# Four token mixers after a two-layer block: the stream kept by token, and the first mixer's branches as a pipeline

## The chip, the cores and the metric

One core of a Trainium2 chip runs the whole program once. The metric is device time in microseconds (us) of one execution. TensorE is PE in the views (PEld is its weight load), VectorE is DVE, ScalarE is ACT, GpSimd is POOL, SyncE (which issues the transfers) is SP.

## What is computed

The program has two parts. The first (two attention and expert layers) is untouched. The second, "block 2", runs four mixers over a stream `h` of 256 tokens with 1024 channels, all in float32:

```
for i in range(4):
    u = rms_norm_2(h, norm_pre[i])
    y = (nsa_mixer, diff_mixer, dilated_mixer, stick_mixer)[i](u, ...)
    h = h + rms_norm_2(y, norm_post[i])
```

Each mixer projects `u` by `w_in` into queries, keys, values and a gate `z`, attends, and returns `(o * silu(z)) @ w_out`. The first (`nsa`) has 16 heads in 4 groups that share keys, and sums three branches per head with weights from a sigmoid gate: attention over 15 compressed blocks, over selected blocks (here all of the causal past) and over a window (here the same).

## The kernel before

**Stream.** `h` lies by channel: tile `xT`, 128 channels x 8 x 256 tokens. `pre` (L317) makes `u = h * gain * r` by channel and splits it into a high and a low half (`uh`, `ul`), since every projection is three products of rounded halves (`gemm`, L261 to L263). The first projections of a mixer (`values`, L568, products L578) don't wait for `u`: they take `raw`, the halves of `h * gain` without the norm's factor (`raw_split`, L303), and scale the result by token (`rc`). A sum of squares by channel goes through small products with a matrix of 1/1024 (L314, L394).

**Weights.** `wload` (L207) brings 256 columns of a matrix, 1 MB, into one of five buffers; `split` (L234) makes two pairs of halves of it, a cast on ScalarE (L248) and a difference on VectorE (L249) each, in a pool of 4 + 4 tiles (`wh`, `wl`), so two chunks at a time. 48 products of 128x128 by 128x256 use one chunk.

**First mixer** (`nsa`, L770). After the keys and values come 4 groups; in each a chunk of queries, then 2 pairs of heads; for a pair two branches, `br` 1 (selected, with the compressed scores in its first 16 columns) and 0 (window). One branch of a pair, called a step here, is: 12 score products (L436), bias and row maximum on VectorE (L928), exponential with row sum on ScalarE (L930), 6 transposes (L465), 2 copies on ScalarE (L467), 4 products with the values (L475, 8 rows in the trace). The weights 1/sum x gate are applied after the products: spread over 64 columns, transposed (L959), copied (L961) and multiplied with the sum (L962). Compressed weights go through L935 to L948 and L967. `gate_split` (L599) makes the four gate chunks, in program order behind the groups.

**End of a mixer.** `out_proj` (L339) multiplies by `w_out` into channels (L350, L385), 192 products; the norm's sums, then by channel pair `y * r`, `h + y` (L411 to L415, VectorE and GpSimd), the next `raw` (L307, L308) and its squares. The last mixer uses `out_last` (L2164), which works by token: rows of `h` come from 16 transposes (L742).

**Order.** Nothing of this is the order on an engine: a scheduler places every instruction ahead of time, so gate products fill gaps of the groups already. PSUM has 8 banks: 2 `mm`, 5 shared by scores and transposes (`x`), 1 `o`.

Of the kernel before, what the change touches and what calls it, by code (L numbers as in the profile page):

```python
# [10 lines left out]
F32 = mybir.dt.float32  # L11
# [8 lines left out]
S = 256  # L20
# [87 lines left out]
class K:  # L108
# [208 lines left out]
    def pre(self, pool, h, gain):  # L317

        nc = self.nc
        if self.raw is None:  # L320
            self.raw_begin(gain)
            for k in range(KT):
                self.raw_split(h, k)
        r = self.rsqrt(pool, self.raw_ps[:, :S], S)
        p = self.pst()
        for t in range(2):
            nc.tensor.matmul(p[:, t:t + 1], r[0:1, 128 * t:128 * t + 128], self.ones[0:1, 0:1], start=True, stop=True)
        rc = pool.tile([128, 2], F32, name="rcol", tag="rcol")
        nc.vector.tensor_copy(rc, p[:, :2])
        u = pool.tile([128, KT, S], F32, name="u", tag="sq")  # L330
        uh = pool.tile([128, KT, S], F32R, name="uh", tag="uh")
        ul = pool.tile([128, KT, S], F32R, name="ul", tag="ul")
        for k in range(KT):
            nc.vector.scalar_tensor_tensor(u[:, k], h[:, k], gain[:, k:k + 1], r, op0=ALU.mult, op1=ALU.mult)
            nc.scalar.copy(uh[:, k], u[:, k])
            (nc.gpsimd if k % 2 else nc.vector).tensor_sub(ul[:, k], u[:, k], uh[:, k].bitcast(F32))
        return (uh, ul), u, rc, r

    def out_proj(self, pool, h, oh, ol, w_out, gain, ahead):  # L339


        nc = self.nc
        y = pool.tile([128, KT, S], F32, name="y", tag="v")
        sq = pool.tile([128, KT, S], F32, name="ysq", tag="sq")
        ps = self.pst()

        def product(p, w, ks):
            for m, k in [(m, k) for m in range(2) for k in ks]:
                for j, (a, b) in enumerate(((1, oh), (0, ol), (0, oh))):
                    nc.tensor.matmul(p[:, 256 * m:256 * m + 256], w[a][k][:, 128 * m:128 * m + 128], b[:, k],  # L350
                                     start=k == 0 and m == 0 and j == 0, stop=k == KT - 1 and m == 1 and j == 2)

        def evict(p, c):
            v = p.rearrange("p (m n) -> p m n", m=2)
            cs = slice(2 * c, 2 * c + 2)
            nc.scalar.activation(sq[:, cs], v, AF.Square)
            nc.vector.tensor_mul(y[:, cs], v, gain[:, cs].unsqueeze(2).to_broadcast([128, 2, S]))
            if 0 < c < 3:
                nc.gpsimd.tensor_add(sq[:, 0:2], sq[:, 0:2], sq[:, cs])

        weights = lambda c: self.wsplit(w_out[:, 256 * c:256 * c + 256], after=self.oh_last if c == 2 else (), pool_too=c == 1)

        ws, p = [weights(0), weights(1)], [self.mm(), self.mm()]
        for ks in ((0, 1, 2, 3), (4, 5), (6, 7)):
            for c in range(2):
                product(p[c], ws[c], ks)
        for c in range(2):
            evict(p[c], c)
        for c in (2, 3):
            w = weights(c)  # L370
            if c == 3 and ahead is not None:
                raw = [self.wload(a) for a in ahead[0]]
                self.ahead = [self.split(raw[0])]
            if c == 2:
                p = self.mm()
                product(p, w, range(KT))
                evict(p, c)
                nc.gpsimd.tensor_add(sq[:, 0], sq[:, 0], sq[:, 1])
            else:

                p = [self.mm()[:, :S], self.pss()[:, :S]]
                for m, ks in ((0, (0, 1, 2, 3)), (1, (0, 1, 2, 3)), (0, (4, 5, 6, 7)), (1, (4, 5, 6, 7))):
                    for k in ks:
                        for j, (a, b) in enumerate(((1, oh), (0, ol), (0, oh))):
                            nc.tensor.matmul(p[m], w[a][k][:, 128 * m:128 * m + 128], b[:, k],  # L385
                                             start=k == 0 and j == 0, stop=k == KT - 1 and j == 2)
                    if ks[0]:
                        k = 6 + m
                        nc.scalar.activation(sq[:, k], p[m], AF.Square)
                        nc.vector.tensor_scalar(y[:, k], p[m], gain[:, k:k + 1], None, op0=ALU.mult)  # L390
        if ahead is not None:
            half = self.split(raw[1][:, :4])
        for j, k in enumerate((0, 6, 7)):
            nc.tensor.matmul(ps[:, :S], self.onesD, sq[:, k], start=j == 0, stop=j == 2)  # L394
        r = self.rsqrt(pool, ps[:, :S], S)
        self.raw = None
        if ahead is not None:
            self.raw_begin(ahead[1])
        last = None

        def then(f):
            nonlocal last
            if last is None:
                last = f()
            else:
                with self.tc.issue_after(last):
                    last = f()

        for i in range(KT + 2):
            if i < KT:  # L410
                then(lambda: nc.vector.tensor_mul(y[:, i], y[:, i], r).ins)  # L411
                if i % 2 == 0:
                    then(lambda: nc.vector.tensor_add(h[:, i], h[:, i], y[:, i]).ins)
                else:
                    nc.gpsimd.tensor_add(h[:, i], h[:, i], y[:, i])  # L415
            j = i - LAG
            if 0 <= j < KT and ahead is not None:
                then(lambda: self.raw_split(h, j))
                if j == AT:
                    with self.tc.issue_after(last):  # L420
                        self.ahead.append([x + y for x, y in zip(half, self.split(raw[1][:, 4:], pool_too=PT))])
# [47 lines left out]
    def spread(self, po, vs, ats):  # L469


        first = None
        for kt, (of, n) in enumerate(((0, 256), (256, 128))):
            for half, (at, _) in enumerate(ats):
                i = self.nc.tensor.matmul(po[64 * half:64 * half + 64, 256 - n:256], vs[half][kt], at[:, of:of + n],  # L475
                                          start=kt == 0, stop=kt == 1).ins
                first = first or i
        self.behind(first, *(i for _, i in ats))

    def diff(self, h, gpre, gpost, ahead=None):  # L480
# [5 lines left out]
        with ExitStack() as ctx:  # L486
# [3 lines left out]
            u, _, rc, _ = self.pre(pool, h, gpre)  # L490
            v = pool.tile([128, 2, D], F32, name="v", tag="v")
            self.values(rc, self.columns256(w_in, 2048, v))
# [16 lines left out]
            for c in range(4):  # L509
                ops = []  # L510
                for base, sc in ((0, 0.125), (1024, 1.0)):
                    w = self.wsplit(w_in[:, base + 256 * c:base + 256 * c + 256])
                    p = self.mm()
                    hi = wk.tile([128, 2, S], F32R, name="qkh", tag=f"qkh{base}")
                    lo = wk.tile([128, 2, S], F32R, name="qkl", tag=f"qkl{base}")
                    for m in range(2):
                        pm = p[:, 256 * m:256 * m + 256]
                        self.gemm_cm(pm, w, m, u)
                        self.split_ps(hi[:, m], lo[:, m], pm, sc)
# [29 lines left out]
            for c in range(4):  # L549
# [5 lines left out]
                self.sigmoid(sz, pz)  # L555
                nc.vector.tensor_mul(sz, sz, pz)
# [8 lines left out]
            self.out_proj(pool, h, oh, ol, w_out, gpost, ahead)  # L565


    def values(self, rc, parts):  # L568

        nc = self.nc  # L570
        x, (last_a, last_b) = self.raw, self.raw_last
        ps = [self.mm(), self.mm()] + (self.pair() if len(parts) > 2 else [])

        def product(i, w, k):
            for t in range(2):
                ts = slice(128 * t, 128 * t + 128)
                for j, (a, b) in enumerate(((0, 1), (1, 0), (0, 0))):
                    nc.tensor.matmul(ps[i][:, 256 * t:256 * t + 256], x[a][:, k, ts], w[b][k], start=k == 0 and t == 0 and j == 0,  # L578
                                     stop=k == KT - 1 and t == 1 and j == 2)

        ws = self.ahead or [self.wsplit(src) for src, _ in parts[:2]]
        self.ahead = None
        for k in range(KT):
            for i in range(2):
                product(i, ws[i], k)
        for i, (src, v) in enumerate(parts):
            if i > 1:
                with self.tc.issue_after(last_a), self.tc.issue_after(last_b):
                    w = self.wsplit(src)
                for k in range(KT):  # L590
                    product(i, w, k)
# [7 lines left out]
    def gate_split(self, wk, w_in, col, x, o, oh, ol, last=None):  # L599

        nc = self.nc
        for c in range(4):
            w = self.wsplit(w_in[:, col + 256 * c:col + 256 * c + 256])
            sz = wk.tile([128, 512], F32, name="sz", tag="sz")
            pz = self.mm()
            for m in range(2):
                self.gemm_cm(pz[:, 256 * m:256 * m + 256], w, m, x)
            self.sigmoid(sz, pz)
# [1674 lines left out]
```

## Time and profile before

| what | us |
|---|---|
| three runs | 1576.27, 1581.42, 1582.22 |
| median of them | 1581.42 |
| the profiled execution, and its span in the trace | 1575.4, 1573.8 |
| PE, DVE, ACT, POOL busy | 1426.8, 974.1, 809.6, 314.5 |
| block 2: first mixer, second, third, fourth | 911 to 1127.5, to 1276, to 1415.5, to 1573.8 |

Busy PE is a share of time in which some product was under way; products overlap, and at the lower clock one takes twice as long and counts as busy too. So the clock that was granted and the distance from product to product are read beside it.

### The profile page before, as it was taken

To read this page: it belongs to the slowest core of one execution; us is meant where nothing else is said; L and a number is where in the kernel's file an instruction comes from. 1 tells how busy PE (TensorE), PEld (TensorE's weight loads), DVE (VectorE), ACT (ScalarE), POOL (GpSimd) and SP (SyncE) were. 2 spreads that over 40 slices of the span, in tenths; PEclk is the share of its full clock that TensorE was granted. 3 is DMA by queue.
4 is the path that set the end of the run, shared out by engine and by line. 5 is a ranking of instruction groups with operands and counts; after the bars stand their busy time and mean duration, and the time that the engine had idled before them with its cause. 6 is when DMAs were issued, how large, how long until landed. Compare 5 with 4: busy or idle time off the path is not lost.

```text
span 1573.8 us, 26604 instructions
## 1 busy us (share of the span) xinstructions
PE 1426.8 (91%) x10361; PEld 1154.0 (73%) x10361; DVE 974.1 (62%) x2043; ACT 809.6 (51%) x1644; POOL 314.5 (20%) x311
## 2 busy tenths in 40 slices
PE   5989987889599898998799999998999989989998
PEld 3767865566477776767466678775899889979997
DVE  4555669863677556875412366553777776768675
ACT  4455454543366544664212344664456755745574
POOL 2000124322211103111000021322321141322242
PEclk8999999999799998999899999995999999999999
DMA  8700259874699987315799937330354454344520
GB/s 266 236 27 3 94 189 291 260 255 149 212 331 341 348 269 266 106 41 185 245 332 366 344 102 219 107 107 1 113 161 134 135 172 150 129 129 153 160 82 27
DMA packets 243689, 284.71 MB, mean 181 GB/s; under 512 B 14546, under 2 KB 227554, under 8 KB 243556
## 3 DMA queue, kind: packets, MB, share of 16 engines
q1 hardware_dynamic: 236644, 259.85, 50.9%
q0 software_dynamic: 6912, 23.07, 4.5%
q8 instruction: 85, 1.39, 0.4%
q14 instruction: 48, 0.39, 0.1%
HBM read 275.56 MB, written 9.44 MB: 181 GB/s over the span
## 4 chain that ended last, share of the span: by engine, by line
PE 43%; ACT 4%; DVE 2%; POOL 1%; issue 1%; another core or an unknown queue 0%; DVEq 0%; ACTq 0%
PE ps_mm L261 6%; PE ps_mm L263 5%; PE ps_mm L262 5%; PE ps_mm L1992 4%; PE ps_mm L350 3%; PE ps_mm L578 2%; PE ps_x L436 2%; PE ps_x L578 2%; PE ps_t L2032 2%; PE ps_o L475 1%; PE ps_t L1975 1%; ACT wh L248 1%; PE ps_x L465 1%; PE ps_s L2037 1%; PE ps_mm L2175 1%
## 5 line engine op out<-in xcount | busy, mean ns | idle before, releaser
L249 DVE TENSOR_TENSOR wl<-w,wh 128x1024 fp32r<-128x1024 f32 x257 | 321.4, 1258 | 147.0 <-ACT wh L248 143.7
L248 ACT CAST wh<-w 128x1024 fp32r<-128x1024 f32 x261 | 270.0, 1042 | 128.2 <-PE ps_mm L263 59.8
L261 PE MATMUL ps_mm<-uh,wl 128*128 128x256 f32 x720 | 209.3, 291 | 0.0
L262 PE MATMUL ps_mm<-ul,wh 128*128 128x256 f32 x720 | 205.5, 285 | 0.0
L263 PE MATMUL ps_mm<-uh,wh 128*128 128x256 f32 x720 | 204.9, 285 | 0.0
L261 PEld LDWEIGHTS ps_mm<-uh,wl 128*128 128x128 f32 x720 | 136.8, 190 | 4.8 <-issue 1.5
L263 PEld LDWEIGHTS ps_mm<-uh,wh 128*128 128x128 f32 x720 | 136.9, 190 | 1.5 <-issue 0.8
L262 PEld LDWEIGHTS ps_mm<-ul,wh 128*128 128x128 f32 x720 | 137.0, 190 | 1.3 <-issue 0.8
L261 PE MATMUL ps_mm<-wh,xl 128*96 128x256 f32 x256 | 75.8, 296 | 3.5 <-DVE xl L427 3.5
L262 PE MATMUL ps_mm<-wl,xt 128*96 128x256 f32 x256 | 74.2, 290 | 0.0
L263 PE MATMUL ps_mm<-wh,xt 128*96 128x256 f32 x256 | 73.1, 286 | 0.0
L1043 PE MATMUL ps_mm<-w,cond 128*32 128x256 f32 x768 | 55.5, 404 | 15.6 <-DVE mod L1050 9.4
L2074 PE MATMUL ps_s<-w,ht 128*96 128x512 f32 x128 | 57.6, 593 | 0.0
L1992 PE MATMUL ps_mm<-w,xt 128*64 128x256 f32 x384 | 51.5, 384 | 0.0
L261 PE MATMUL ps_mm<-hh,wl 128*128 128x512 f32 (+2 forms) x136 | 47.5, 351 | 2.9 <-DVE qn L1087 2.6
L1043 PEld LDWEIGHTS ps_mm<-w,cond 128*32 128x32 f32 x768 | 22.2, 113 | 37.4 <-DVE mod L1050 12.4
L313 POOL TENSOR_TENSOR rawsq<-rawsq 128x256 f32<-128x256 f32 x16 | 13.7, 857 | 176.7 <-ACT rawsq L312 176.6
L350 PE MATMUL ps_mm<-oh,wl 128*128 128x256 f32 x144 | 42.5, 302 | 6.9 <-DVE sz L609 2.9
L261 PEld LDWEIGHTS ps_mm<-wh,xl 128*96 128x96 f32 x256 | 42.7, 167 | 7.7 <-DVE xl L427 4.5
L262 PE MATMUL ps_mm<-hl,wh 128*128 128x512 f32 (+2 forms) x136 | 47.3, 348 | 0.3 <-DVE hl L1068 0.2
L263 PE MATMUL ps_mm<-hh,wh 128*128 128x512 f32 (+2 forms) x136 | 46.8, 344 | 0.0
L1489 POOL TENSOR_TENSOR xk<-d,KD 128x512 f32<-128x512 f32 x27 | 39.8, 1481 | 33.6 <-PE ps_x L1496 13.2
(654 smaller groups left out, 3998.1 us busy)
## 6 DMA issues: line engine op xcount, KB each, us to landing
w<-mod_w SPq DMA_DIRECT2D x48, 1024.0 KB, 7.3
w<-exp_w_up SPq DMA_DIRECT2D x28, 1024.0 KB, 10.6
w<-exp_w_gate SPq DMA_DIRECT2D x27, 1024.0 KB, 11.9
w<-exp_w_down SPq DMA_DIRECT2D x27, 1024.0 KB, 11.3
w<-b_w_in SPq DMA_DIRECT2D x16, 1024.0 KB, 5.6
w<-d_w_in SPq DMA_DIRECT2D x16, 1024.0 KB, 5.4
w<-a_w_in SPq DMA_DIRECT2D x14, 1024.0 KB, 8.3
w<-c_w_in SPq DMA_DIRECT2D x14, 1024.0 KB, 5.0
```

The source lines that it names most:

```text
L248: nc.scalar.copy(hv, raw[:, i:i + c])
L249: (nc.gpsimd if i and pool_too else nc.vector).tensor_sub(lv, raw[:, i:i + c], hv.bitcast(F32))
L261: nc.tensor.matmul(out, sl(k), mh(k), start=k == ks[0], stop=False)
L262: nc.tensor.matmul(out, sh(k), ml(k), start=False, stop=False)
L263: nc.tensor.matmul(out, sh(k), mh(k), start=False, stop=k == ks[-1])
L350: nc.tensor.matmul(p[:, 256 * m:256 * m + 256], w[a][k][:, 128 * m:128 * m + 128], b[:, k], start=k == 0 and m == 0 and j == 0, stop=k == ...
L436: self.nc.tensor.matmul(out, q[a], k[b], start=j == 0, stop=j == 2)
L578: nc.tensor.matmul(ps[i][:, 256 * t:256 * t + 256], x[a][:, k, ts], w[b][k], start=k == 0 and t == 0 and j == 0, stop=k == KT - 1 and t == ...
L1043: nc.tensor.matmul(p[j:j + 32, :256], self.cond[:, k], w[:, k], start=k < 4, stop=k >= 4)
L1489: nc.gpsimd.tensor_mul(xk, d, Ks)
L1992: nc.tensor.matmul(p[64 * a:64 * a + 64, 256 * j:256 * j + 256], xt[:, k, off + 64 * a:off + 64 * a + 64], w[j][a][k], start=k == 0, stop= ...
L2074: nc.tensor.matmul(p, ht[:, f], w[:, f, cs], start=f == 0, stop=f == 1)
```

## The change

Block 2 keeps `h` by token (`self.h`, filled by 16 transposes inside the first mixer, `rows_of`). `pre`, `u` and its halves are gone: all projections take `raw`, and the norm's factor is multiplied into each result on VectorE (`normed`), from PSUM, before the split. The output product lies by token in all four mixers; `out_last` is merged into `out_proj`. There each token tile (128 tokens) has its own chain: norm, sum, 8 transposes, and the halves of 128 columns at a time for the next mixer. In `nsa` a step's weights are scaled by 1/sum x gate on VectorE before they are turned, so both branches, both pairs and the compressed part add up in one bank (`po[g]`), which is multiplied by the gate once. The steps are written as a pipeline, scores of the next ahead of the transposes of this one, and each group has its gate chunk inside. `gain` of the output norm is now a row, loaded for each mixer.

```diff
+    def norm_first(self):
+        nc.scalar.activation(self.rr, self.raw_ps[:, :S], AF.Ln, bias=self.eps)
+        nc.scalar.activation(self.rr, self.rr, AF.Exp, scale=-0.5)
         p = self.pst()
         for t in range(2):
+            nc.tensor.matmul(p[:, t:t + 1], self.rr[0:1, 128 * t:128 * t + 128], self.ones[0:1, 0:1], start=True, stop=True)
...
+    def normed(self, wk, p, r, n=2):
+        t = wk.tile([128, n, S], F32, name="normed", tag="normed")
+        self.nc.vector.tensor_mul(t, p[:, :n * S].rearrange("p (m n) -> p m n", m=n), r[:, None, :].to_broadcast([128, n, S]))
...
+    def split_normed(self, wk, hi, lo, p, r):
+        t = self.normed(wk, p, r)
+        self.nc.scalar.copy(hi, t)
+        self.nc.vector.tensor_sub(lo, t, hi.bitcast(F32))
...
+    def out_proj(self, pool, oh, ol, w_out, gain, ahead=None, out=None):
...
+        def add(t, b):
+            nc.vector.scalar_tensor_tensor(dst[:, t, cs], y[:, t, cs], r[:, t:t + 1], h[:, t, cs], op0=ALU.mult, op1=ALU.add)
...
+            for k in range(4):
+                nc.tensor.transpose(p[:, 128 * k:128 * k + 128], h[:, t, 512 * b + 128 * k:512 * b + 128 * k + 128], self.ident)
+            for k in range(4):
+                i = nc.scalar.mul(hi, v, g)
+                j = nc.vector.scalar_tensor_tensor(lo, v, g, hi.bitcast(F32), op0=ALU.mult, op1=ALU.subtract)
...
+        w = weights(3)
         if ahead is not None:
+            self.ahead = [self.wsplit(a) for a in ahead[0]]
...
+        for t in range(2):
+            product(p, t, 3, w, range(KT))
+            evict(p, t, 3)
+            norm(r[:, t:t + 1], ssq[:, t])
+            for b in range(2):
+                add(t, b)
+            if ahead is not None:
+                for b in range(2):
+                    nc.scalar.activation(junk, h[:, t, 512 * b:512 * b + 512], AF.Square, accum_out=hsq[:, t, b:b + 1])
+                norm(rc[:, t:t + 1], hsq[:, t])
...
+            def weigh(g, m, br):
...
+                nc.vector.reciprocal(sm, sm)
+                nc.vector.tensor_mul(sm, sm, gt[:, :, 1 + br, 4 * g + 2 * m:4 * g + 2 * m + 2])
+                for half, e in enumerate(es):
+                    for t, (of, n) in enumerate(spans):
+                        nc.vector.tensor_scalar(e[:, of:of + n], e[:, of:of + n], sm[:, t, half:half + 1], None, op0=ALU.mult)
+                return es
...
+            steps = [(g, m, br) for g in range(4) for m in range(2) for br in (1, 0)]
+            queries(0)
+            es = weigh(*steps[0])
+            for i, (g, m, br) in enumerate(steps):
+                nxt = weigh(*steps[i + 1]) if i + 1 < len(steps) else None
+                add(g, m, br, es)
+                es = nxt
+                if (m, br) == (0, 1):
+                    sz[g] = self.gate(wk, w_in[:, 2608 + 256 * g:2864 + 256 * g])
+                if (m, br) == (0, 0) and g < 3:
+                    queries(g + 1)
+                if (m, br) == (1, 1):
+                    self.rows_of(h, g // 2, g % 2)
```

Two places show what the scheduler makes of it. The first is PE at the end of the first mixer's groups. Before, from the sixth step before the last, nothing stands between the steps:

```order
L465 MATMUL ps_x<-k_all,e 128x128 x6
L475 MATMUL ps_o<-at,vsw 64x256 x2
L475 MATMUL ps_o<-at,vsw 64x128 x2
L946 MATMUL ps_x<-k_all,sc 64x128 x2
L436 MATMUL ps_x<-KH,ql 128x128 x2
L436 MATMUL ps_x<-KL,qh 128x128 x2
L436 MATMUL ps_x<-KH,qh 128x128 x2
L436 MATMUL ps_x<-KH,ql 128x256 x2
L436 MATMUL ps_x<-KL,qh 128x256 x2
L436 MATMUL ps_x<-KH,qh 128x256 x2
L465 MATMUL ps_x<-k_all,e 128x128 x6
L475 MATMUL ps_o<-at,vsw 64x256 x2
```

With the change (L453 are scores, L482 transposes, L492 value products) the last such place is three steps long and ends with output products (L350):

```order
L492 MATMUL ps_o<-at,vsw 64x128 x2
L482 MATMUL ps_x<-k_all,e 128x128 x4
L453 MATMUL ps_x<-KH,ql 128x128 x2
L453 MATMUL ps_x<-KL,qh 128x128 x2
L453 MATMUL ps_x<-KH,qh 128x128 x2
L453 MATMUL ps_x<-KH,ql 128x256 x2
L453 MATMUL ps_x<-KL,qh 128x256 x2
L453 MATMUL ps_x<-KH,qh 128x256 x2
L482 MATMUL ps_x<-k_all,e 128x128 x2
L350 MATMUL ps_mm<-wl,oh 128x256 x2
L350 MATMUL ps_mm<-wh,ol 128x256
```

Query and gate products, which fill the gaps, now stand among 13 of the 16 steps, and 56 output products among the last two. Between the first scores and the last step's value products stand 275 gate and query products and 56 output products (before 315 and 41); 40 more of the former stand ahead of the first scores.

The second place is DVE where one mixer ends and the next begins, behind the last output products. Before, channel by channel:

```order
L411 TENSOR_TENSOR y<-y,rs 128x256
L413 TENSOR_TENSOR xT<-xT,y 128x256
L308 SCALAR_TENSOR_TENSOR rawl<-xT,cols_mix,rawh 128x256
L249 TENSOR_TENSOR wl<-w,wh 128x1024
L411 TENSOR_TENSOR y<-y,rs 128x256
L308 SCALAR_TENSOR_TENSOR rawl<-xT,cols_mix,rawh 128x256
L411 TENSOR_TENSOR y<-y,rs 128x256
L413 TENSOR_TENSOR xT<-xT,y 128x256
```

With the change (`hrow` is the stream by token):

```order
L249 TENSOR_TENSOR wl<-w,wh 128x1024
L366 SCALAR_TENSOR_TENSOR hrow<-y,rout,hrow 128x512 x2
L249 TENSOR_TENSOR wl<-w,wh 128x1024
L378 SCALAR_TENSOR_TENSOR rawl<-ps_x,cols_mix,rawh 128x128
L359 TENSOR_REDUCE rc<-hsq 128x1
L378 SCALAR_TENSOR_TENSOR rawl<-ps_x,cols_mix,rawh 128x128
L356 TENSOR_TENSOR y<-ps_x,gain 128x256
L359 TENSOR_REDUCE rout<-ssq 128x1
L378 SCALAR_TENSOR_TENSOR rawl<-ps_x,cols_mix,rawh 128x128 x3
L366 SCALAR_TENSOR_TENSOR hrow<-y,rout,hrow 128x512 x2
L378 SCALAR_TENSOR_TENSOR rawl<-ps_x,cols_mix,rawh 128x128 x2
```

The two differences `wl` there belong to the second chunk of the next mixer's weights; their buffers are those of the last chunk of `w_out`, so the second of them can only start when the last output product is done, and the first halves of the new stream stand behind it.

In the third mixer (`dilated`) the order now has all 288 query and key products ahead of the first scores and all 192 gate products ahead of the second half of the heads; 48 output products are left between that half's last scores and its first transposes, where 72 gate and 48 output products stood.

## Rows read from the trace of the kernel before

**Rows 1.** Busy time by stretch: start:end, us, PE, PEld, DVE, ACT, POOL, granted clock, DMA share, GB/s

```profile
911.00:1127.50 216.50, 196.80 (x1478) 168.37 (x1478) 125.21 (x348) 117.04 (x281) 53.47 (x62) 0.88 0.34 106
1127.50:1276.00 148.50, 141.99 (x1141) 133.41 (x1142) 109.77 (x228) 95.49 (x200) 32.87 (x28) 1.00 0.45 144
```

**Rows 2.** The same view, the groups of the first mixer in parts and whole

```profile
972.00:1060.00 88.00, 80.64 (x681) 70.16 (x682) 52.36 (x185) 57.69 (x154) 24.17 (x24) 0.97 0.33 103
1060.00:1094.90 34.90, 28.28 (x142) 17.68 (x138) 13.26 (x70) 14.03 (x47) 8.52 (x9) 0.55 0.07 23
971.80:1106.50 134.70, 120.64 (x897) 98.55 (x896) 71.02 (x265) 76.30 (x213) 32.89 (x33) 0.85 0.23 74
```

**Rows 3.** Chain that ended last, the first mixer's groups: start, us, what

```profile
978.23 0.91 PE ps_x L436 x12
1049.68 0.80 PE ps_o L475 x8
1059.70 1.55 PE ps_o L475 x8
1089.39 1.55 PE ps_o L475 x8
1104.17 0.80 PE ps_o L475 x8
```

**Rows 4.** The same chain, from one mixer to the next, and two short pieces

```profile
1003.14 1.02 PE ps_x L967 x4
1122.41 1.44 PE ps_x L385 x12
1143.80 11.51 PE ps_x L578 x96
1270.68 1.44 PE ps_x L385 x12
1293.82 13.02 PE ps_x L578 x96
1358.31 0.33 PE ps_x L465 x3
1569.32 0.75 DVE y L2206
```

**Rows 5.** Timeline of ACT where the first mixer begins: start, us, line, what

```profile
918.53 0.47 ACT L285 ACTIVATE rs<-ps_t,eps 128x256 f32<-128x256 f32 x1 [2.15 <-PE ps_t L314]
919.03 0.42 ACT L286 ACTIVATE rs<-rs 128x256 f32<-128x256 f32 x1
```

**Rows 6.** The same view of PE, the first value product

```profile
917.93 0.78 PE L578 MATMUL ps_mm<-wl,rawh 128*128 128x256 f32 x1
```

**Rows 7.** The same view of SP (its DMA issues), from there on

```profile
915.44 0.47 SPq L782 DMA_DIRECT2D w<-a_cmp_w_v  x1
929.25 0.37 SPq L220 DMA_DIRECT2D w<-a_cmp_w_k  x1
```

**Rows 8.** The page's costliest groups: busy us, mean ns, idle before and releaser

```profile
L249 DVE TENSOR_TENSOR wl<-w,wh 128x1024 fp32r<-128x1024 f32 x257 | 321.4, 1258 | 147.0 <-ACT wh L248 143.7
L248 ACT CAST wh<-w 128x1024 fp32r<-128x1024 f32 x261 | 270.0, 1042 | 128.2 <-PE ps_mm L263 59.8
```

**Rows 9.** Groups by form, first mixer, 911 to 1127.5

```profile
L962 DVE TENSOR_TENSOR rs<-ps_o,rs 128x512 f32<-128x512 f32 x8 | 5.5, 688 | 10.4 <-ACT rs L961 9.5 <-PE ps_o L475 0.8
L429 ACT ACTIVATE qh<-ps_mm 128x256 fp32r<-128x256 f32 x8 | 3.1, 384 | 3.5 <-PE ps_x L436 2.2 <-PE ps_mm L263 1.1
L950 DVE RECIPROCAL sm<-sm 128x8 f32<-128x8 f32 x8 | 1.6, 203 | 5.9 <-ACT e L930 5.9
L952 DVE TENSOR_TENSOR sm<-sm,gt 128x8 f32<-128x8 f32 x8 | 1.3, 167 | 0.3
L972 DVE TENSOR_TENSOR o<-o,ps_x 128x512 f32<-128x512 f32 x3 | 2.1, 686 | 2.5 <-POOL o L963 2.5
```

**Rows 10.** Groups by form on DVE, the other three mixers, 1127 to 1574

```profile
L357 DVE TENSOR_TENSOR y<-ps_mm,cols_mix 128x512 f32<-128x512 f32 x6 | 4.1, 687 | 4.0 <-ACT ysq L356 4.0
L537 DVE TENSOR_SCALAR e<-e,rc 128x256 f32<-128x256 f32 x8 | 3.0, 378 | 0.0
L538 DVE SCALAR_TENSOR_TENSOR e<-e,rc 128x128 f32<-128x128 f32 x8 | 2.8, 344 | 0.0
L537 DVE TENSOR_SCALAR e<-e,rc 128x128 f32<-128x128 f32 x8 | 2.3, 287 | 0.2
```

**Rows 11.** Busy time by stretch, end of the third mixer

```profile
1376.00:1400.00 24.00, 19.08 (x133) 17.60 (x132) 15.35 (x39) 11.27 (x21) 3.64 (x2) 0.93 0.36 112
```

More of the change, by code (lines that the diff above doesn't have):

```diff
@@ L325, in pre @@
         p = self.pst()
         for t in range(2):
[L327 to L336, printed above, removed]
@@ L365, in out_proj @@
             for c in range(2):
[L366 to L390, printed above, removed]
@@ L391, in out_proj @@
-        if ahead is not None:
[L392 to L421, printed above, removed]
+                for t in range(2):
+                    product(p, t, c, ws[c], ks)
@@ new lines, in out_proj @@
+        for t in range(2):
+            for c in range(2):
+                evict(p, t, c)
+        p = [self.pss(), self.pss()]
+        w = weights(2)
+        for t in range(2):
+            product(p, t, 2, w, range(KT))
+            evict(p, t, 2)
+        w = weights(3)
+        if ahead is not None:
+            self.ahead = [self.wsplit(a) for a in ahead[0]]
+            self.raw = [x.tile([128, KT, S], F32R, name=n, tag=n) for x, n in ((self.rawh, "rawh"), (self.ub, "rawl"))]
+            rc = self.hp.tile([128, 2], F32, name="rc", tag="rc")
@@ new lines, in out_proj @@
+        for t in range(2):
+            product(p, t, 3, w, range(KT))
[7 more added lines that the diff above has]
+                norm(rc[:, t:t + 1], hsq[:, t])
+        if ahead is None:
+            return
+        rb = pool.tile([128, 2, 128], F32, name="rb", tag="ysq")
@@ L564, in diff, with values, product @@
                 self.gated(c, o, sz, oh, ol)
-            self.out_proj(pool, h, oh, ol, w_out, gpost, ahead)
-    def values(self, rc, parts):
+            self.out_proj(pool, oh, ol, w_out, gain, ahead)
+    def values(self, parts):
         nc = self.nc
-        x, (last_a, last_b) = self.raw, self.raw_last
+        x, (last_a, last_b), rc = self.raw, self.raw_last, self.rc
         ps = [self.mm(), self.mm()] + (self.pair() if len(parts) > 2 else [])
[L574 to L581, printed above, removed]
-        self.ahead = None
-        for k in range(KT):
-            for i in range(2):
-                product(i, ws[i], k)
+        def product(i, w, t, k):
+            ts = slice(128 * t, 128 * t + 128)
+            for j, (a, b) in enumerate(((0, 1), (1, 0), (0, 0))):
+                nc.tensor.matmul(ps[i][:, 256 * t:256 * t + 256], x[a][:, k, ts], w[b][k], start=k == 0 and t == 0 and j == 0,
+                                 stop=k == KT - 1 and t == 1 and j == 2)
+        ws = self.ahead
+        self.ahead = None
+        tiles = range(2)
+        order = ([(i, t, k) for t in tiles for i in range(2) for k in range(KT)] if self.by_tile else
+                 [(i, t, k) for k in range(KT) for i in range(2) for t in tiles])
+        for i, t, k in order:
+            product(i, ws[i], t, k)
         for i, (src, v) in enumerate(parts):
@@ L589, in values @@
                     w = self.wsplit(src)
-                for k in range(KT):
-                    product(i, w, k)
+                for t in tiles:
+                    for k in range(KT):
+                        product(i, w, t, k)
             nc.scalar.mul(v[:, 0], ps[i][:, :256], rc[:, 0:1])
@@ new lines, in add @@
+            def add(g, m, br, es):
+                if br and m == 0:
+                    po[g] = self.pso()
+                ats = [self.turn_causal(wk, e) for e in es]
+                self.spread(po[g][:, 256 * m:256 * m + 256], [[vsw[:, br, kt, 64 * g:64 * g + 64] for kt in range(2)]] * 2, ats, br == 1 and m == 0, False)
+                if br or m == 0:
+                    return
+                blocks(g)
+                for c in (slice(0, 256), slice(256, 512)) if g == 3 else (slice(0, 512),):
+                    ks = slice(2 * g + c.start // 256, 2 * g + c.stop // 256)
+                    nc.vector.tensor_mul(o[:, ks].rearrange("p m n -> p (m n)"), po[g][:, c], sz[g][:, c])
```

382 lines of the change are left out of this document (169 added, 213 removed).

## Prediction

> **What bounds the kernel now.** First comes busy time by stretch. In block 2's second mixer PE is busy 142 of 148.5 us at a granted clock of 1.00, so PE is the bound there; in the first it is busy 197 of 216.5 at 0.88 [rows 1]. The first mixer is therefore read in parts. Up to 1060 us its groups run well: 80.6 of 88 us busy (0.92), clock 0.97. From 1060 to 1095 PE is busy 28.3 of 34.9 with 142 products, and the clock is 0.55, near the lower of its two levels, 1.2 GHz [rows 2]. The order says why the filling is missing: the gate products are used up. The chain of waits gives the price: the value products of four steps lie between the ends of those at 1059.70 and 1089.39, 29.7/4 = 7.4 us a step, and such a set takes 1.55 us where it takes 0.80 at full clock [rows 3]. Then the chain is read where a mixer ends. Its last output products end at 1122.41 + 1.44 = 1123.85 and the next first value products start at 1143.80: 19.95 us. The next time it is 1272.12 to 1293.82, 21.7 [rows 4]. With 96 such products in 11.51 us, one is 0.12 us; I take 20.8 for each of the three transitions.
>
> All that follows is summed against the profiled execution, 1575.4 us (its span is 1573.8). The median of the runs shown is 6 us above it.
>
> **The change, part by part.**
>
> *Start of the first mixer.* Two one-column products now stand on PE ahead of the first value products and wait for the two ScalarE steps of the norm, which end at 919.45 [rows 5]. Behind them all of PE waits, where the first value product began at 917.93 [rows 6]. I take +1.5 us; 1 if the steps are reached sooner, 3 if the copy behind them matters. On SP the new gain row stands ahead of three weight loads. There SP has idle time from 915.9 to 929.25 [rows 7], so a wait for the end of ScalarE's work of part one costs nothing; if that cover were gone, the loads behind it would come late by what the wait exceeds 13 us.
>
> *Groups.* 40 query and gate products go ahead of the first scores, which moves their start from 978.23 [rows 3] by 40 x 0.12 = 4.8 and the 1.5 to 984.5. PE's own work from there to the last step: 275 + 56 = 331 products x 0.12 = 39.7; 16 score sets x 0.91 = 14.6 [rows 3]; 120 transposes (96 of steps, 8 compressed, 16 of the stream) x 0.33/3 = 13.2; 16 value sets x 0.80 = 12.8; four compressed sets x 1.02 = 4.1 [rows 3, 4]. Sum 84.4, and at the busy share of the good part, 0.92 [rows 2], 91.7 us. Three unfilled steps remain at the end. There a step can't be shorter than VectorE's work for it (below, 91/16 = 5.7) nor need it be longer than today's 7.4; I take 6, against PE's own 2.4, so 3 x 3.5 = 10.5 more. The groups take 102 us and end at 1086.5. (Today, 126.7 from the first scores to the last value products.)
>
> VectorE in those groups has 71.0 us now [rows 2]. It gains 64 scalings of weights, which I price by the same operation in the third mixer, 32 x (0.378 + 0.287) = 21.3; six norm products at 0.687, 4.1 [rows 10]; twice the reciprocals and gate weights, 8 x (0.203 + 0.167) = 3.0; four copies of rows and four gate products of 128x512 at 0.69, 5.5 [rows 9]. It loses eight weighted products, 5.5, and about five sums of 0.69, 3.4 [rows 9], and four weight differences of 1.258, 5.0 [rows 8]. That is 91: below 102, so VectorE sets the unfilled steps alone. The bounds are 92 (no unfilled loss) and 16 x 7.4 = 118 (every step as slow as today's unfilled ones).
>
> Behind the groups stand 192 - 56 = 136 output products, 16.3 us, and 0.5 for the last gate product: they end at 1103.3, where they ended at 1123.85. **-20.5.**
>
> *Transitions.* Call the end of the last output product T. The second chunk's first weight buffers come free 12 products before T, so cast and difference end at T - 1.4 + 1.04 + 1.25 = T + 0.9 [rows 8]. Behind it are two additions of 0.75 (price of the last mixer, which already works by token) [rows 4], then the second difference of 1.25, whose buffer comes free only at T: T + 3.65. Then 16 halves of 128x128, priced by the nearest form, 0.344 [rows 10], 5.5; the second tile's additions 1.5, its eviction and the reductions 1.2, so T + 11.9 for the last half. The first value products run under this from about T + 4. Some 30 remain behind it, 3.5 us, and 1 is lost to the next chunk's cast: what took 20.8 + 11.5 ends at T + 16.4 + 11.5. Gain 4.4 a transition, **-13.2** for three. Bounds for one: 15.5 (all products hidden) and 22.5.
>
> The upper bound is a sharing of banks. In the trace the eviction on VectorE already waits for ScalarE's squares of the same tile, 4.0 us for six [rows 10]. The new halves have ScalarE (0.384 for a larger form [rows 9]) and VectorE both read one tile of transposes. If they go strictly one after another, a token tile's eight pairs take 8 x (0.384 + 0.344) = 5.8 us instead of 2.7 paced by VectorE, +3.1 a tile, 16.4 + 6.2 = 22.6 a transition: nothing is gained. The Trainium skill, page "PSUM — Partial Sum Buffer", section "PSUM bank collisions raise a hardware error", says that two engines, ScalarE and VectorE too, may not touch one bank at one time; the wait on the squares agrees with it. By that rule alone the sum would have 0 in place of -13.2. I take 16.4, since the order places other VectorE work between the halves of one tile, so ScalarE can run ahead there.
>
> *Third mixer.* Between the second half's scores and its transposes 48 products (5.8 us) stand instead of 120. Around that place PE is busy 19.1 of 24 us now [rows 11]; I take +2, bounds -2 (nothing waits, the gates fill elsewhere) and +6.
>
> *Small parts.* Fourth mixer: its 16 transposes of the stream move out (16 x 0.11 = -1.8), with them some filling: 0, bounds -3 and +4. Evictions: squares and gain product no longer wait for each other on two tiles of both later transitions, 0.7 each (4.0/6) [rows 10]: -1.4. The norm of the gates (0.69) precedes their sigmoid; the early output products hide all but 0.5: +0.5. The removed `u` and its halves lie beside full PE, as does the normed split that replaces them: 0; uncovered, it would be 0.69 a chunk. Three gain rows of 512 KB lie under a DMA share of 0.34 to 0.45 [rows 1]: 0.
>
> Sum: -20.5 - 13.2 + 2 + 0 - 1.4 + 0.5 = -32.6, so 1542.8 from 1575.4, or 1548.8 from the median. I state **1546**; rivals are counted from there.
>
> **Rivals.** (a) *The chain of the steps binds.* VectorE and ScalarE go through a step in order (bias and maximum, exponential, scaling, turn), and scaling lengthens the chain by 2 x (0.378 + 0.287) + 0.37 = 1.7 us a step; then all 16 steps take 7.4, 118 instead of 102: 1562. For: today's unfilled steps; against: in the filled part PE was busy 0.92, so its products and not the chain paced those ten steps, and the pipeline overlaps two steps. (b) *The transitions give nothing* (one bank, or VectorE's longer queue): 1559. (a) and (b) together: 1575. (c) *The pipeline isn't one*: the scores of the next step wait for banks, and six unfilled steps remain: 3 x 3.5 more, 1556. (d) *Slower: the clock.* Filling is now spread evenly; PE's share would be 84/102 = 0.83, close to the 0.81 (28.3/34.9) of the stretch at 0.55 and below the 0.92 of that at 0.97 [rows 2]. If a share f of the groups runs at 1.2 GHz, PE's 84 us double there: +84 f. It decides, more than 0.5% slower, from 84 f = 32.6 + 7.9, f = 0.48; at f = 0.6 it gives 1596. Against it: filled steps with output or gate products between all short pieces held 0.97 today.
>
> **How the numbers follow.** Forecast 0.52, (a) 0.13, (b) 0.12, both 0.05, (c) 0.06, (d) 0.09; 0.03 for a small loss I don't see. The line of 0.5%, 7.9 us, is about what a measurement of this kernel can tell from no change. Faster: forecast, (a), (b), (c), 0.83; same: both and the rest, 0.08; slower: (d), 0.09. The range runs from 1524 (groups 10 us shorter, transitions 1 us shorter each, third and fourth mixer at their low ends, -7, and 2 for the spread of runs: 22) to 1569 (above (a), with the third mixer's +4); outside lie both together, (d), and little else.
>
> **What would show it.** Right: clock near 1.0 in the first mixer's groups; groups of about 102 us with only the last three steps unfilled; last output product of the first mixer near 1103; the 96 first value products starting near T + 4 and done 28 us after T, where now it is 32; VectorE about 91 us in the groups. Wrong: value sets of 1.55 us over many steps (d); steps of 7 us with PE idle behind ScalarE's turns (a); halves of the stream waiting for ScalarE, with more than 20 us lost (b); stalls of PE above 6 us in the third mixer.

## The result and the profile after

| | before | with the change |
|---|---|---|
| median of four runs each, us | 1578.85 | 1558.63 |
| ratio, 95% interval | | 0.988 [0.984, 0.991] |
| profiled execution, span | 1575.4, 1573.8 | 1558.01, 1555.9 |
| block 2: from the start of the last squares of part one, which both kernels have, to the end of the span | 1157.4 | 1136.5 |
| start of these squares | 916.40 | 919.42 |
| first scores, end of the groups | 978.16, 1104.98 | 989.47, 1086.92 |
| last output product of mixers 1 to 4: its start and 0.12, the distance from one product to the next | 1123.7, 1271.9, 1411.0, 1567.5 | 1108.7, 1259.2, 1393.1, 1549.4 |
| from there to the products of the third chunk of values | 20.1, 21.8, 20.9 | 17.7, 16.9, 17.2 |

The change is faster by 1.2%. In the two traces it takes 20.9 us out of block 2; part one, which it doesn't touch, ends 3.0 us later in this profile. Rows of the timeline of PE behind these times, before and then after:

```profile
916.40 2.09 PE L314 MATMUL ps_t<-rawsq,onesD 128*128 128x256 f32 x4 [0.72 <-POOL rawsq L313]
978.16 0.33 PE L436 MATMUL ps_x<-KH,ql 64*128 64x144 f32 x2
1123.55 0.28 PE L385 MATMUL ps_x<-oh,wh 128*128 128x256 f32 x1
```

```profile
919.42 2.09 PE L314 MATMUL ps_t<-rawsq,onesD 128*128 128x256 f32 x4 [0.77 <-POOL rawsq L313]
922.52 1.01 PE L325 MATMUL ps_t<-ones,rr 1*128 1x1 f32 x4 [1.01 <-ACT rr L322]
923.46 0.58 PE L590 MATMUL ps_mm<-wl,rawh 128*128 128x256 f32 x1
989.47 0.34 PE L453 MATMUL ps_x<-KH,ql 64*128 64x144 f32 x2
1101.40 0.39 PE L350 MATMUL ps_x<-wl,oh 128*128 128x256 f32 x1 [2.78 <-DVE y L356]
1108.57 0.28 PE L350 MATMUL ps_x<-wh,oh 128*128 128x256 f32 x1
1126.37 0.28 PE L590 MATMUL ps_x<-wl,rawh 128*128 128x256 f32 x1
```

The groups answer to [rows 2]. Busy time by stretch after (columns as there): first the groups whole, then their filled part and their end, then the last 48 output products of the first mixer and the first value products of the second:

```profile
989.40:1087.00 97.60, 95.29 (x786) 80.35 (x785) 78.27 (x329) 66.82 (x195) 20.22 (x15) 0.97 0.25 80
988.00:1060.00 72.00, 72.00 (x627) 62.15 (x626) 62.53 (x260) 52.16 (x154) 14.32 (x12) 1.00 0.31 100
1060.00:1087.00 27.00, 24.69 (x172) 19.54 (x171) 17.14 (x70) 15.71 (x44) 5.89 (x3) 0.87 0.13 40
1101.40:1108.60 7.20, 7.20 (x48) 7.20 (x48) 0.81 (x4) 1.89 (x5) 0.00 (x0) 0.76 0.53 160
1112.50:1117.10 4.60, 4.54 (x26) 4.54 (x27) 3.94 (x14) 4.21 (x18) 0.00 (x0) 0.63 0.80 246
```

The groups fell from 126.8 to 97.5 us, at clock 0.97 instead of 0.85 (which [rows 2] give over a slightly wider stretch). But the fourth row is new: 48 output products, 5.7 us at full clock, take 7.2 at 0.76, and the timeline shows PE idle 2.78 us just ahead of them. One row for each of the four mixers, from the groups by form on PE, says what ended that idle time:

```profile
L350 PE MATMUL ps_x<-wl,oh 128*128 128x256 f32 x32 | 9.8, 305 | 2.8 <-DVE y L356 2.8
L350 PE MATMUL ps_x<-wl,oh 128*128 128x256 f32 x32 | 9.8, 306 | 3.1 <-DVE y L356 3.1
L350 PE MATMUL ps_x<-wl,oh 128*128 128x256 f32 x32 | 9.9, 309 | 3.1 <-DVE y L356 3.1
L350 PE MATMUL ps_x<-wl,oh 128*128 128x256 f32 x32 | 9.1, 286 | 2.3 <-DVE y L356 2.3
```

`y` at L356 is the eviction of the third 256 columns. The fourth 256 lie in the same two banks (L350 writes the other half of `p[t]`), so PE waits for it. ScalarE and VectorE around 1099 show what makes it late in the first mixer: casts (L248) and differences (L249) of the next mixer's weights stand ahead of it.

```profile
1097.23 1.05 ACT L248 CAST wh<-w 128x1024 fp32r<-128x1024 f32 x1 [0.26 <-PE ps_x L350]
1098.66 1.04 ACT L248 CAST wh<-w 128x1024 fp32r<-128x1024 f32 x1
1099.61 0.38 ACT L355 ACTIVATE ysq<-ps_x 128x256 f32<-128x256 f32 x1
...
1098.32 1.23 DVE L249 TENSOR_TENSOR wl<-w,wh 128x1024 fp32r<-128x1024 f32 x1 [0.55 <-ACT wh L248]
1099.79 1.22 DVE L249 TENSOR_TENSOR wl<-w,wh 128x1024 fp32r<-128x1024 f32 x1
1100.92 0.75 DVE L356 TENSOR_TENSOR y<-ps_x,gain 128x256 f32<-128x256 f32 x2
```

Before, the first three mixers gave these columns other banks (L385 writes `ps_mm` and `ps_x`). The fourth had the shared form already, and its row before was there to be read:

```profile
L2175 PE MATMUL ps_x<-wl,oh 128*128 128x256 f32 x32 | 9.1, 283 | 1.3 <-DVE y L2181 1.3
```

### The profile page after: what moved, and what is told of

Same layout as the page of the kernel before. It is cut to its first block, busy times and chain, and to the rows that moved or that the text cites. A ratio compares the mean times of both kernels' runs of the same rounds, so it can differ in the third digit from the quotient of the medians.

```text
span 1555.9 us, 26545 instructions
## 1 busy us (share of the span) xinstructions
PE 1414.0 (91%) x10345; PEld 1149.8 (74%) x10345; DVE 966.7 (62%) x2107; ACT 807.0 (52%) x1665; POOL 253.6 (16%) x245
## 5 line engine op out<-in xcount | busy, mean ns | idle before, releaser
L249 DVE TENSOR_TENSOR wl<-w,wh 128x1024 fp32r<-128x1024 f32 x258 | 314.0, 1225 | 165.2 <-ACT wh L248 163.7
L248 ACT CAST wh<-w 128x1024 fp32r<-128x1024 f32 x262 | 270.1, 1040 | 182.4 <-PE ps_mm L263 101.8
L261 PE MATMUL ps_mm<-rawh,wl 128*128 128x256 f32 x720 | 206.0, 286 | 0.0
L262 PE MATMUL ps_mm<-rawl,wh 128*128 128x256 f32 x720 | 205.6, 286 | 0.0
L263 PE MATMUL ps_mm<-rawh,wh 128*128 128x256 f32 x720 | 204.7, 284 | 0.0
L263 PEld LDWEIGHTS ps_mm<-rawh,wh 128*128 128x128 f32 x720 | 136.7, 190 | 2.8 <-issue 1.6
L261 PEld LDWEIGHTS ps_mm<-rawh,wl 128*128 128x128 f32 x720 | 136.0, 189 | 2.5 <-issue 0.7
L262 PEld LDWEIGHTS ps_mm<-rawl,wh 128*128 128x128 f32 x720 | 136.2, 189 | 1.6 <-issue 0.6
L1070 PEld LDWEIGHTS ps_mm<-w,cond 128*32 128x32 f32 x768 | 22.7, 115 | 39.6 <-issue 13.6
L350 PE MATMUL ps_x<-wl,oh 128*128 128x256 f32 x128 | 38.6, 301 | 11.2 <-DVE y L356 11.2
L262 PEld LDWEIGHTS ps_mm<-wl,xt 128*96 128x96 f32 x256 | 42.9, 168 | 0.8 <-issue 0.8
## 6 DMA issues: line engine op xcount, KB each, us to landing
w<-exp_w_gate SPq DMA_DIRECT2D x27, 1024.0 KB, 11.6
```

The source lines that it names most:

```text
L248: nc.scalar.copy(hv, raw[:, i:i + c])
L249: (nc.gpsimd if i and pool_too else nc.vector).tensor_sub(lv, raw[:, i:i + c], hv.bitcast(F32))
L261: nc.tensor.matmul(out, sl(k), mh(k), start=k == ks[0], stop=False)
L262: nc.tensor.matmul(out, sh(k), ml(k), start=False, stop=False)
L263: nc.tensor.matmul(out, sh(k), mh(k), start=False, stop=k == ks[-1])
L350: nc.tensor.matmul(p[t][:, 256 * (c % 2):256 * (c % 2) + 256], o[:, k, 128 * t:128 * t + 128], w[b][k], start=k == 0 and c != 1 and j == 0 ...
```

## The experiments

Two questions: which part of the change shortens the groups, and what the new wait costs. All medians are to be held against 1558.6 with the change and 1575.5 to 1579.4 before, on the chips of the runs.

**The pipeline taken out.** 

```diff
-                nxt = weigh(*steps[i + 1]) if i + 1 < len(steps) else None
                 add(g, m, br, es)
-                es = nxt
...
+                es = weigh(*steps[i + 1]) if i + 1 < len(steps) else None
```

> The changed kernel with the scores of the next step written behind the transposes and value products of this one. The order on PE then has eight steps with filling and seven at the end with none, where the changed kernel has three of them at most. Theory A (what the pipeline brings is that the filling lasts: an unfilled step costs 3 to 4 us more than PE's own work and lowers the clock): four to five more unfilled steps, 15 to 20 us longer groups, 1573 to 1579 us. Rival B (VectorE's 80 us in the groups pace all steps alike): the groups stay within 4 us of 97, 1558 to 1563.

1588.7 us, 1.007 [1.005, 1.009] of before: theory A, and above its range by 10 us. The groups take 127.6 us, as long as before the change (126.8), at clock 0.76:

```profile
994.00:1122.00 128.00, 113.53 (x782) 89.35 (x781) 81.50 (x329) 68.10 (x195) 18.92 (x15) 0.76 0.19 61
```

**The pipeline alone**, in the kernel before; the rest of its groups is unchanged, but for one buffer of `rs` instead of two and four of the weights `e` instead of three, as two steps are now under way at once. (The run without the pipeline has four of them too, and 127.6 us.) The steps' bodies became two functions, `weigh` and `add`; of that only the loop is shown:

```diff
...
+            steps = [(g, m, br) for g in range(4) for m in range(2) for br in (1, 0)]
+            es = weigh(*steps[0])
+            for i, (g, m, br) in enumerate(steps):
+                nxt = weigh(*steps[i + 1]) if i + 1 < len(steps) else None
+                add(g, m, br, es)
+                es = nxt
```

> The kernel before, with nothing but its 16 steps written as a pipeline (scores, bias and exponential of the next step ahead of the turn of this one); the weights are still applied to the products, the gates stand behind the groups, the stream lies by channel. The order on PE has filling up to the last steps. Theory A (the pipeline is what shortens the groups, scaling and gates have no part in it): groups of 97 to 102 us instead of 126.8, 1549 to 1554 us. Rival B (one bank for the sums of a pair, which the chain of weights, their turn, copy and product empties: the next pair's value products wait for it, and the scaling ahead of the turn is needed too): groups of 108 us or more, 1560 or above.

1548.4 us, 0.982 [0.979, 0.986]: theory A's time, with groups even shorter than its 97 to 102 us, and 10 us less than the whole change. Groups of 94.2 us, PE busy throughout at full clock; the one bank holds nobody up:

```profile
978.00:1078.00 100.00, 100.00 (x873) 87.35 (x872) 72.68 (x262) 74.30 (x213) 33.03 (x32) 1.00 0.28 86
```

So the pipeline is the whole gain in the groups, and in block 2 it is worth more alone (1157.4 to 1124.1) than with the rest of the change (1136.5).

**The gates behind the groups again.** 

```diff
-                if (m, br) == (0, 1):
-                    sz[g] = self.gate(wk, w_in[:, 2608 + 256 * g:2864 + 256 * g])
...
+            self.gate_split(wk, w_in, 2608, o, oh, ol)
```

> The changed kernel with the gate products written behind the groups, as before the change, and the summed branches copied out of their bank and multiplied with the gate later. The order on PE still has gate products among 13 of the steps. Theory A (it is the pipeline, not the place of the gates in the program, that spreads the filling): groups within 4 us of 97, and up to 3 us at their end for the gate products on VectorE and GpSimd that now follow: 1558 to 1563 us. Rival B (the gates inside are what fills the last steps): the steps at the end run empty, 10 us or more, 1569 or above.

1553.9 us, 0.984 [0.981, 0.988], below theory A's 1558 to 1563; the interval overlaps that of the change. Rival B is out. The groups take 94.1 us, and the slow steps at their end are gone; the place of the gates in the program fills nothing. Whether it does harm is taken up below.

```profile
992.00:1086.00 94.00, 93.78 (x802) 80.11 (x802) 82.18 (x329) 66.50 (x195) 23.57 (x18) 1.00 0.27 84
```

**Each weight scaled twice.**

```diff
+                        nc.vector.tensor_scalar(e[:, of:of + n], e[:, of:of + n], 1.0, None, op0=ALU.mult)
```

> The changed kernel with each of the 64 scalings of weights followed by a second one, by 1.0: 32 x (0.358 + 0.307) = 21 us more on VectorE, in the middle of each step's chain. Theory A (VectorE has room, 80 of 97 us are busy, and PE paces the filled steps): the first 17 us of it are free and the unfilled last steps grow by 1.3 each: the groups take 102 to 106 us, 1563 to 1568 us. Rival B (the in-order chain through VectorE paces the groups already): all 21 us show, 1578 to 1582.

1566.7 us, 0.992 [0.990, 0.994]: theory A. The groups take 105.0 us, 7.5 more, for operations priced at 21 us one by one; they overlap, and VectorE's busy time in the groups rose by 13.0 (from 78.27).

```profile
994.70:1099.70 105.00, 98.86 (x782) 82.31 (x782) 91.23 (x393) 67.66 (x195) 20.41 (x15) 0.90 0.23 74
```

**Own banks for the last 256 columns.**

```diff
+        p = [self.pss(), self.pss()]
         for t in range(2):
             product(p, t, 3, w, range(KT))
```

> The changed kernel, with two banks of their own for the last 256 columns of the output product. In the changed kernel's trace PE stands still 2.8 to 3.1 us ahead of these products in each of the first three mixers, and 2.3 in the last, released by the eviction of the 256 columns before, which lie in the same banks; behind it the products run at half clock for a while (48 products take 7.3 us instead of 5.7). Theory A (the shared bank is what makes PE wait, and the eviction is late because VectorE has weight differences ahead of it): the four idle stretches go and the half clock with them, 3 x 4.6 + 2, about 1543 us, at most 1548. Rival B (PE is early there in any case: the chain eviction, norm, addition, new halves sets the start of the next mixer): the idle stretch moves behind the last output product, the time from there to the next mixer's products grows by as much, 1555 to 1559.

1542.7 us, 0.979 [0.975, 0.982]: the size of theory A, but not quite its place. The wait for the eviction is gone in all four mixers. In its stead PE waits 2.6, 2.5 and 2.5 us for the new stream, since the order now has the first tile's turn ahead of 24 output products:

```profile
1103.09 1.29 PE L372 MATMUL ps_x<-k_all,hrow 128*128 128x128 f32 x8 [2.59 <-DVE hrow L366]
```

These 24 products then cover the making of the new halves, and from the last one to the third chunk of values it is 13.6, 13.4 and 13.4 us instead of 17.7, 16.9 and 17.2, of which 11.5 are products. Block 2 takes 1121.6 us, 14.9 less than with the change, for the reckoned 3 x 4.6 + 2. In the first mixer the clock of the stretches that answer to the fourth row above is full:

```profile
1092.00:1100.30 8.30, 8.30 (x72) 8.30 (x70) 6.32 (x10) 6.74 (x16) 0.00 (x0) 1.00 0.70 228
1103.10:1107.00 3.90, 3.87 (x32) 3.66 (x33) 2.23 (x7) 3.52 (x13) 0.00 (x0) 1.00 0.45 157
```

In the second and third it is not: behind their waits of 2.49 and 2.50 us the clock is 0.78 from 1250.0 to 1254.0 and 0.80 from 1379.8 to 1384.0, the stretches of the 24 products. So the half clock went with the wait in one mixer of three. And since a wait of this length is left, the run shows what separate banks are worth in this order, not the price of the old wait by itself; that price is read from the next two runs.

**Shared banks, the eviction first.** First on VectorE alone:

```diff
+            self.evicted = nc.vector.tensor_mul(y[:, t, cs], v, gain[:, cs]).ins
...
-            self.ahead = [self.wsplit(a) for a in ahead[0]]
+            raws = [self.wload(a) for a in ahead[0]]
+            with self.tc.issue_after(self.evicted):
+                self.ahead = [self.split(a) for a in raws]
```

> The changed kernel with its shared banks, but the halves of the next mixer's weights issued behind the evictions of the third 256 columns, which on VectorE stand behind two weight differences in the changed kernel. Theory A (the bank is shared, but what makes the wait 3 us long is VectorE's order): the idle stretch ahead of the last 256 columns falls from 3 us to under 1 in the first three mixers and the half clock behind it goes; the next weights come a little later: 1546 to 1551 us. Rival B (the bank itself costs it: a chain of square and product after the last product of a tile, whatever stands ahead): the stretch stays above 2 us, 1555 or above.

1556.6 us, 0.987 [0.983, 0.992]. The wait is 1.97, 2.47 and 2.48 us: by its numbers this is rival B, but for the 1.97. Its reason, the bank alone, is not shown by that: the gain products now stood first on VectorE, and waited for squares that still stood behind two casts on ScalarE, the second of them here:

```profile
1101.16 1.04 ACT L248 CAST wh<-w 128x1024 fp32r<-128x1024 f32 x1
1102.11 0.38 ACT L355 ACTIVATE ysq<-ps_x 128x256 f32<-128x256 f32 x1
...
1102.61 0.93 DVE L356 TENSOR_TENSOR y<-ps_x,gain 128x256 f32<-128x256 f32 x2 [0.99 <-ACT ysq L355]
```

Then on both (`squared` is the square's instruction, as `evicted` is the gain product's):

```diff
-            with self.tc.issue_after(self.evicted):
+            with self.tc.issue_after(self.evicted), self.tc.issue_after(self.squared):
```

> As the run before with the evictions first, now on ScalarE too: there the casts of the next mixer's weights stood ahead of the squares of the third 256 columns, and the idle stretch of PE was still 2.0 to 2.5 us with the gain products waiting for those squares. Theory A (the wait is the queue of next weights ahead of the eviction on both engines, and the shared bank only makes PE feel it): the first tile is evicted under the second tile's products, the stretch is under 0.5 us and the half clock behind it is gone: 1545 to 1549 us. Rival B (sharing the bank costs PE a wait whatever the order): above 1.5 us remain, 1553 or above.

1549.7 us, 0.984 [0.982, 0.986]; 0.68, 1.46 and 1.45 us are left. In the first mixer, and in the fourth:

```profile
1096.78 0.38 PE L350 MATMUL ps_x<-wl,oh 128*128 128x256 f32 x1 [0.68 <-DVE y L356]
1531.89 0.39 PE L350 MATMUL ps_x<-wl,oh 128*128 128x256 f32 x1 [2.33 <-DVE y L356]
```

Block 2 takes 1127.1 us, 9.4 less than with the change and 5.5 more than with own banks. The clock behind these waits is 1.00 in the first three mixers. So more than half of the wait there, 2.1, 1.6 and 1.6 us, is the queue of next weights ahead of the eviction. That is nearer theory A, which put the rest under 0.5. The rest must have another reason: the fourth mixer has no next weights and still waits 2.3 us in all these orders. On ScalarE and VectorE the evictions of the first 512 columns stand ahead there; no run moves them. With own banks PE waits for none of them.

**Repairs together.** The first tile's turn issued behind the second tile's last products, on own banks:

```diff
...
+        with self.tc.issue_after(self.last_product):
+            turn(0, 0)
+        for t in range(2):
+            rest(t)
```

> The kernel with own banks for the last 256 columns, and the first token tile's turn on PE held behind the second tile's last products. With own banks alone PE waits 2.5 us for the first tile's new stream in each transition while 24 output products stand behind the turn. Theory A (only the place on PE is wrong): those products fill the wait and about 1 us is left of it behind the last product, 3 x 1.5: 1537 to 1540 us. Rival B (the chain eviction, norm, addition, turn, halves is as long as the products put ahead of it, and each of its later steps comes later): no gain, 1541 to 1545.

1543.7 us, 0.978 [0.974, 0.982], block 2 1121.6 us as with own banks: rival B. The wait moves behind the last product as 1.7 + 0.8 us.

Own banks and the gates behind, the two diffs above:

> Own banks for the last 256 columns and the gate products written behind the groups, together. Theory A (the two gains lie in different stretches and add): 1542.7 - 4.7 = 1538 us, 1535 to 1541. Rival B (the 4.7 us of the gates behind came from chance among runs): 1541 to 1545.

1542.0 us, 0.978 [0.975, 0.981]: rival B's range. The groups keep their 94.1 us, the median is that of own banks; whether the gates' place is worth anything stays open.

All three:

> Own banks, gates behind the groups, and the first tile's turn behind the second tile's last products. If all add: 1533 to 1537 us. If the place of the turn gives nothing: as with the first two alone, 1536 to 1540.

1539.3 us, 0.976 [0.973, 0.979], in the range in which the turn's place gives nothing; the fastest here, and not told apart from the two before.

And with the norm's columns later:

```diff
...
             product(i, ws[i], t, k)
+        if not self.by_tile:
+            self.norm_cols()
```

> All three repairs together, and the two one-column products of the first norm behind the first value products instead of ahead of them. From the last sum of squares to the first value product PE waits 4.0 us in the changed kernel and 1.5 in the one before. If the wait is only the place on PE: 2.5 us less there, 1536 to 1538 us. If the first values then wait for the norm at their end: no change, 1538 to 1541.

1540.4 us, 0.976 [0.972, 0.981], no change: the first value product follows the squares after 2.7 us instead of 4.0, and nothing of it is seen in the time.

## Why the prediction was right, and where it was not

The time lies in the range and on the side forecast, but with 20 us gained, where 32.6 were forecast, it is near rivals (a) and (b), for a reason neither names. By its steps, predicted and measured in block 2, against [rows 2 to 4]:

| step | predicted | measured |
|---|---|---|
| first value product | +1.5 | +2.5 |
| products ahead of the first scores | +4.8 | +5.8 |
| groups (126.8 before) | 102 | 97.5 |
| end of the groups to the last output product (18.7) | 16.8 | 21.8 |
| three transitions | -13.2 | -11.0 |
| second mixer, values to last output product | -0.7 | +4.6 |
| third | +1.3 | -0.3 |
| fourth, to the end | +0.5 | +3.7 |
| sum | -32.6 | -20.9 |

*Groups: the right reason, with sizes that made up for each other.* Three unfilled steps at the end and the clock near full, as forecast, and 97.5 us where 102 stood. That they end at 1086.9, with 1086.5 forecast, is luck: the start is 5 us later than forecast (3.0 of it from part one) and the groups 4.5 shorter. Inside the term, too, two sizes were off. In the filled part PE was busy 72.00 of 72.00 us, not 0.92 of it, and rival (d) was wrong: the clock stayed at 1.00 there. PE's own work was more than the 84.4 reckoned: taking from 97.5 us the 2.3 of idle time and the 3.5 lost to the clock in the last 27 us (at 0.87) leaves 92, an estimate from the rows above. The unfilled end cost these 5.8 us, not 10.5. VectorE was set too high, 91 us against 78.3: the base, 71.0, came from a wider stretch (67.1 from the first scores on), and the 64 scalings, at the mean price taken, overlap and fill 17.0 us instead of 21.3; the two make 8.2 of the 12.7. The group on VectorE after:

```profile
L947 DVE TENSOR_SCALAR e<-e,sm 128x128 f32<-128x128 f32 x64 | 17.0, 333 | 0.3
```

That pipelining alone does it, and scaling and inner gates don't, the prediction could not tell; the two runs on the pipeline show it.

*Evictions: the step that failed.* The term took 0.7 us off two evictions, -1.4, since square and gain product no longer wait for each other. It did not ask which bank the next product writes. The last 256 columns share it with the columns being evicted, the eviction stands behind the next mixer's weights on two engines, and PE waits 2.8 to 3.1 us and then runs 48 products in 7.2 to 7.3 us instead of 5.7: 4.5 a mixer in three mixers, and 1.0 more in the fourth than before (2.3 against 1.3). That is 14.5 us where -1.4 stood. The eviction-first run bears out the cause and the larger part of the size: 2.1, 1.6 and 1.6 us of wait and three times 1.5 of half clock are gone, 9.8 together, and block 2 is 9.4 shorter, with transitions as long as with the change (17.8, 17.5, 16.9). Own banks bring back 14.9; that this comes so near 14.5 is in part chance, since they leave a wait of 2.5 to 2.6 us and gain 4.0, 3.6 and 3.9 us in the transitions. In the table the failed step is in the fourth row and the sixth, and hidden in the seventh and eighth.

*Transitions: nearly right.* 17.3 us instead of the 16.4 worked out. One sentence of the prediction is wrong: the products at 1143.80 are not the first value products but those of the third and fourth chunk of values. The 96 of the first two start at 1127.60 (T + 3.9) in the trace before and run inside the 20 us, as its own count then has it. With the change they start at T + 3.0, 2.4 and 2.9. VectorE's queue came out as reckoned: the last half is done at T + 11.9, 11.7 and 11.6, with T + 11.9 forecast. What was set too short is the rest, 5.8, 5.2 and 5.7 us instead of 4.5: in the first transition 48 products are left there, where 30 and a cast were reckoned. Part of that is clock: the stretch from T + 3.8 on, the last of the five above, ran 4.6 us at 0.63. Rival (b) was wrong: a pair of halves takes 0.4 us, between VectorE's 0.34 and the 0.73 of strict turns. ScalarE and VectorE after, seven pairs each:

```profile
1117.41 2.83 ACT L377 ACTIVATE rawh<-ps_x,cols_mix 128x128 fp32r<-128x128 f32 x7
...
1117.91 2.70 DVE L378 SCALAR_TENSOR_TENSOR rawl<-ps_x,cols_mix,rawh 128x128 fp32r<-128x128 f32 x7
```

The two engines overlap there, from 1117.91 to 1120.24. The trace does not tell whether they do so in one bank or take turns in the two that hold the transposes of a token tile. Either way the rule that two engines may not touch one bank at a time (the Trainium skill, "PSUM — Partial Sum Buffer", section "PSUM bank collisions raise a hardware error") did not cost the transitions what rival (b) reckoned. The trace agrees with it at another place: PE's writes into one half of a bank stand behind the eviction's reads of the other half, 2.78 us in the first mixer, and with own banks that wait is gone.

*Third and fourth mixer.* The third lost 4.6 us to wait and half clock and still came out level, so about 5 us were gained elsewhere in it, where +2 was forecast. Its first 36 us ran at clock 1.00 instead of 0.95, which is 1.8 us of them; the rest stays open. In the fourth, beside the 1.0 of the eviction, 1.5 us are waits for GpSimd's tiles (L778), from which filling went, and 1.6 for the gated halves ahead of the output products (L645). The trace before has neither wait there. The bound of +4 allowed for this.

*Small terms.* The gain row cost nothing: its load was issued at 919.23, and SP's next at 934.39, 15 us later. The first two one-column products cost 2.5, inside the bounds; moving them brought no measurable gain.

## What to carry to other kernels

When output columns are cut anew, list for each product which bank it writes and whose eviction has to be through, and what stands ahead of that eviction on each engine; two more banks were worth 16 us here, more than half of the 29 that the pipeline gave. A change of many parts wants each part alone: one part, the pipeline, was faster than the whole. Even with own banks block 2 takes 1121.6 us, 2.5 less than with the pipeline alone, so the rest of the change, the stream by token above all, brought little in this form; no run has it alone. Where another place of the program already has the new form, read its waits first.

## What was not expected of the hardware

The clock after a short stop of PE. In the kernel with the change, 48 products ran at 0.76 behind 2.78 us of waiting. With own banks the clock was 1.00 behind 2.59 us in the first mixer, but 0.78 and 0.80 behind 2.49 and 2.50 in the next two. With the eviction first on VectorE 48 products took 5.7 us behind 1.97 us, but 7.3 behind 2.47. And part one, the same program throughout, ended between 916.4 and 926.3 us in the profiles of these kernels, so single times were compared from its end on.
